# Norm 2's squares summed over four channel blocks on GpSimd before the matmul with ones, and the down product's operands loaded a step earlier through six places

## The chip, the cores and the metric

One core of a Trainium2 chip runs the kernel. The metric is the device time of one execution in microseconds, from three runs of it. Within the core, TensorE (PE; its weight loads are listed apart as PEld), VectorE (DVE), ScalarE (ACT) and GpSimd (POOL) each work through a list of instructions in order; SyncE (SP) issues nearly all DMA transfers, also in order, so a transfer whose place on the chip is not free yet holds back every transfer listed behind it.

## The reference

The reference is one inference step of a hybrid layer on 640 tokens, 128 of context and 512 latent ones, in float32, with D = 2048 channels and a feed-forward width of 5632:

```
h  = rmsnorm(x, norm1_g) * (1 + sc1) + sh1
p  = h @ w_in
o_a, state = bidirectional RWKV-7 scan over p's first part
o_b = chunked gMLP over the rest
x  = x + g1 * (concat(o_a, o_b) @ w_out)
h  = rmsnorm(x, norm2_g) * (1 + sc2) + sh2            # norm 2
ff = (silu(h @ w_ffn_gate) * (h @ w_ffn_up)) @ w_ffn_down
y  = final rmsnorm(x + g2 * ff)
```

where `rmsnorm` divides a token's channels by the root of the mean of their squares. The three outputs are both token streams after the last norm, and the context's scan states. The change touches norm 2 and the last of the products, `@ w_ffn_down`, called the down product here.

## The kernel before, in words

**Products.** Channels lie on partitions and tokens along the free axis. Every float32 operand of a product is split in two: ACT copies the rounded high part (`hi`, L1329 and L163), DVE subtracts it from the operand for the low part (`lo`, L1330 and L164), and TensorE does three matmuls for each 128x128 block of weights: hi by hi, hi by lo, lo by hi (L1511 to L1513 in the feed-forward part, L1364 to L1366 for `w_out`). In the feed-forward part the products are done Strassen's way. For each 2x2 block of weights there are seven products of sums of blocks, taken in the order 1, 2, 3, 7, 5, 6, 4 (`PORD`). GpSimd makes the sums of weights (`combine`, L1424).

**Order of the work.** The kernel is written in a framework whose scheduler sets each engine's order of instructions; buffers are named places in pools, and a load into a place waits until the last reader of what stood there is done.

**Norm 2.** Ahead of it, the product with `w_out` is done for two halves of 320 tokens (`hf`), and within each for 16 blocks m of 128 output channels. A block takes 24 matmuls; then `add_out` (L1012) puts the result into `x1T[m]`, a DMA stores it, ACT squares it (L1375), and one block later TensorE multiplies the squares by a matrix of ones and adds them up in PSUM (`stats`, L1348), 16 times for each half. Each of these calls to `TE.matmul` has two float32 operands and appears as two MATMUL records. At m = 15 `stats` forms the norm's factor `rs` (L1351 to L1353). While the second half is being multiplied, `first_half` applies `rs` to the first: GpSimd multiplies (L1300), DVE scales and shifts (L1302), and the operands of the up product are split (L1290, L1291).

**Up product.** It goes over the blocks f of the feed-forward width, `ORDER` having `NFF` of them, two by two. Each pair's gated activations are stored to HBM as the down product will need them: the sums 1, 2, 7 and 6 whole in `d_op`, the sums 3, 5 and 4 already split in `d_os`.

**Down product.** It runs in six chunks of the feed-forward width (`CHK` = 3, 3, 4, 4, 4 and 4 pairs of blocks) with eight steps n each, a step being the seven products for one pair of output blocks. The seven operands `xd` of a chunk stay on the chip for its eight steps. At the last step of each chunk, called the **turn** here (the end of the up product for chunk 0), `load_ops` brings in the next chunk's operands: `direct` (L1550) loads operands 3, 5 and 4, which are split already; `load` (L1556) loads the others into `opd` tiles of up to two blocks, which go through four places (`stags`), and `part` then splits them, copies on ACT (L1563) and subtractions on DVE (L1564; on GpSimd for the block in `POOLK`). An operand's old `xd` tiles are in use until its product in the turn is done, so a new operand can be put in only behind that product. The steps at which this happens are in `AT` and `BT`: operands 1 and 2 are loaded at product index o = 1 of the turn, 1 is put in and 7 loaded at o = 2, 2 is put in and 6 loaded at o = 4, 7 is put in at o = 6, and 6 at o = 0 of the next chunk's first step. The weights `rawd` (L1535) are loaded two steps ahead through ten places (`wtags`); all of these places are on the same queue, SP's.

## Time and profile before

| | us |
|---|---|
| three runs | 3448.01, 3428.27, 3420.05 |
| median of the runs | 3428.27 |
| the profiled execution, its own time | 3418.51 |
| its span, from the first to the last instruction | 3416.7 |
| PE busy | 3253.2 (95% of the span) |
| DVE busy | 2413.6 (71%) |
| ACT busy | 1449.3 (42%) |
| GpSimd busy | 1239.6 (36%) |

The last four rows are busy times over the whole program and hide that its stages have different limits. The parts that the change touches are two: norm 2, from 1561 to 1690 us of the span, and the six turns, of which the first lies at 2786 to 2812 us and the last at 3245 to 3265. The profile's rows name engine, line, operation and tiles: `lo L1330` is the subtraction that writes the tile `lo` on line 1330. An x and a number is a count, and a tile name ahead of `<-` is what is written.

### The profile page before, as it was taken

To read this page: it belongs to the slowest core of one execution; us is meant where nothing else is said; L and a number is where in the kernel's file an instruction comes from. 1 tells how busy PE (TensorE), PEld (TensorE's weight loads), DVE (VectorE), ACT (ScalarE), POOL (GpSimd) and SP (SyncE) were. 2 spreads that over 40 slices of the span, in tenths; PEclk is the share of its full clock that TensorE was granted. 3 is DMA by queue.
4 is the path that set the end of the run, shared out by engine and by line. 5 is a ranking of instruction groups with operands and counts; after the bars stand their busy time and mean duration, and the time that the engine had idled before them with its cause. 6 is when DMAs were issued, how large, how long until landed. Compare 5 with 4: busy or idle time off the path is not lost.

```text
span 3416.7 us, 72586 instructions
## 1 busy us (share of the span) xinstructions
PE 3253.2 (95%) x28260; PEld 2934.0 (86%) x28260; DVE 2413.6 (71%) x4320; ACT 1449.3 (42%) x3161; POOL 1239.6 (36%) x1090
## 2 busy tenths in 40 slices
PE   6899999999999999999899999999999999999996
PEld 3688777777877887768899999999999999999986
DVE  4547766765866666654887768777777777877787
ACT  3334444434444333323554444444444444443365
POOL 0001121112112103230136565656565655555543
PEclk8899999999999999999999999999999999999998
DMA  8766676766667587644533444343434354543453
GB/s 318 236 186 186 183 190 179 174 173 179 175 185 198 152 251 221 207 143 143 168 116 112 124 121 126 106 127 115 130 103 130 116 173 151 155 148 116 144 167 114
DMA packets 736176, 550.11 MB, mean 161 GB/s; under 512 B 140328, under 2 KB 670008, under 8 KB 727000
## 3 DMA queue, kind: packets, MB, share of 16 engines
q1 hardware_dynamic: 723512, 531.78, 52.3%
q0 software_dynamic: 9984, 13.13, 1.8%
q8 instruction: 222, 3.64, 0.4%
q14 instruction: 122, 1.00, 0.1%
q10 hardware_dynamic: 2336, 0.57, 0.1%
HBM read 436.68 MB, written 111.28 MB: 160 GB/s over the span
## 4 chain that ended last, share of the span: by engine, by line
PE 45%; DVE 4%; issue 4%; DMA 1%; POOL 0%; ACT 0%; DVEq 0%; SPq 0%; POOLq 0%; ACTq 0%
PE P L1513 14%; PE P L1511 14%; PE P L1512 14%; DVE lo L1330 1%; DMA opd<-d_op 1%; DVE xd L1564 1%; PE big L1366 0%; PE big L1364 0%; PE big L1365 0%; DVE xo L1291 0%; DVE out L1867 0%; PE C L1445 0%; PE C L1443 0%; PE C L1444 0%; POOL rawd L1424 0%
## 5 line engine op out<-in xcount | busy, mean ns | idle before, releaser
L1511 PE MATMUL P<-xo,hi 128*128 128x320 f32 x2352 | 727.7, 309 | 3.3 <-ACT hi L1329 3.3
L1513 PE MATMUL P<-xo,lo 128*128 128x320 f32 x2352 | 727.4, 309 | 1.9 <-DVE lo L1330 1.9
L1512 PE MATMUL P<-xo,hi 128*128 128x320 f32 x2352 | 727.4, 309 | 0.0
L1330 DVE TENSOR_TENSOR lo<-raw,hi 128x512 fp32r<-128x512 f32 x532 | 509.1, 960 | 177.1 <-ACT hi L1329 172.3
L1329 ACT CAST hi<-raw 128x512 fp32r<-128x512 f32 x532 | 330.7, 622 | 495.4 <-PE P L1512 399.1
L185 PE MATMUL big<-h_hi,hi 128*128 128x320 f32 x1376 | 456.3, 332 | 9.5 <-ACT hi L163 4.5
L1511 PEld LDWEIGHTS P<-xo,hi 128*128 128x128 f32 x2352 | 442.1, 188 | 3.5 <-ACT hi L1329 3.5
L1513 PEld LDWEIGHTS P<-xo,lo 128*128 128x128 f32 x2352 | 441.9, 188 | 2.3 <-DVE lo L1330 2.3
L187 PE MATMUL big<-h_hi,lo 128*128 128x320 f32 x1376 | 442.9, 322 | 0.7 <-DVE lo L164 0.7
L186 PE MATMUL big<-h_lo,hi 128*128 128x320 f32 x1376 | 441.8, 321 | 0.5 <-DVE h_lo L342 0.5
L1512 PEld LDWEIGHTS P<-xo,hi 128*128 128x128 f32 x2352 | 442.1, 188 | 0.0
L1424 POOL TENSOR_TENSOR raw<-raw 128x512 f32<-128x512 f32 x252 | 409.3, 1634 | 12.7 <-DVE lo L1330 1.1
L1513 PE MATMUL P<-xd,lo 128*128 128x320 f32 x1232 | 385.3, 313 | 17.6 <-DVE lo L1330 17.4
L1511 PE MATMUL P<-xd,hi 128*128 128x320 f32 x1232 | 383.2, 311 | 6.0 <-ACT hi L1329 2.6
L1512 PE MATMUL P<-xd,hi 128*128 128x320 f32 x1232 | 381.9, 310 | 0.0
L164 DVE TENSOR_TENSOR lo<-raw,hi 128x512 fp32r<-128x512 f32 x268 | 185.1, 693 | 247.9 <-ACT hi L163 225.0
L185 PEld LDWEIGHTS big<-h_hi,hi 128*128 128x128 f32 x1376 | 266.8, 194 | 83.3 <-issue 55.2
L163 ACT CAST hi<-raw 128x512 fp32r<-128x512 f32 x268 | 165.4, 619 | 302.5 <-PE big L186 142.6
L186 PEld LDWEIGHTS big<-h_lo,hi 128*128 128x128 f32 x1376 | 267.2, 194 | 17.9 <-issue 12.3
L187 PEld LDWEIGHTS big<-h_hi,lo 128*128 128x128 f32 x1376 | 266.8, 194 | 12.2 <-issue 4.8
L1329 ACT CAST hi<-rawd 128x512 fp32r<-128x512 f32 (+1 forms) x288 | 168.8, 587 | 239.0 <-PE P L1512 203.7
L1513 PEld LDWEIGHTS P<-xd,lo 128*128 128x128 f32 x1232 | 232.4, 189 | 25.5 <-DVE lo L1330 25.3
(358 smaller groups left out, 6288.3 us busy)
## 6 DMA issues: line engine op xcount, KB each, us to landing
wt<-in_w_mod_dram SPq DMA_DIRECT2D x96, 1024.0 KB
raw<-in_w_ffn_gate_dram SPq DMA_DIRECT2D x182, 256.0 KB
raw<-in_w_ffn_up_dram SPq DMA_DIRECT2D x182, 256.0 KB
rec<-d_S SPq DMA_DIRECT2D x80, 576.0 KB
raw<-in_w_in_dram SPq DMA_DIRECT2D x172, 256.0 KB
rawd<-in_w_ffn_down_dram SPq DMA_DIRECT2D x128, 256.0 KB
raw<-in_w_out_dram SPq DMA_DIRECT2D x96, 256.0 KB
xd<-d_os SPq DMA_DIRECT2D x66, 320.0 KB
```

What stands on the lines that cost most here:

```text
L163: S.copy(hi, raw)
L164: V.tensor_sub(lo, raw, hi.bitcast(F32))
L185: TE.matmul(halves[hf], hi[:, k, :], h_hi[:, kb, s], start=(kb == 0), stop=False)
L186: TE.matmul(halves[hf], hi[:, k, :], h_lo[:, kb, s], start=False, stop=False)
L187: TE.matmul(halves[hf], lo[:, k, :], h_hi[:, kb, s], start=False, stop=(kb == KB - 1))
L1329: S.copy(hi[:, 0:nk], raw[:, 0:nk])
L1330: V.tensor_sub(lo[:, 0:nk], raw[:, 0:nk], hi[:, 0:nk].bitcast(F32))
L1424: G.tensor_tensor(out=o[:, 0:nk], in0=p[:, 0:nk], in1=q[:, 0:nk], op=ALU.subtract)
L1511: TE.matmul(ps, hi[:, k, :], xk[:, 0, :], start=f, stop=False)
L1512: TE.matmul(ps, hi[:, k, :], xk[:, 1, :], start=False, stop=False)
L1513: TE.matmul(ps, lo[:, k, :], xk[:, 0, :], start=False, stop=l)
L1564: (G if (k + q) in POOLK else V).tensor_tensor(out=x[:, 1, :], in0=t[:, q, :], in1=x[:, 0, :].bitcast(F32), op=ALU.subtract)
```

## The change

**Norm 2.** `squares` squares a block as before, but adds it on GpSimd to the sum of the blocks before it in its group, and only the group's sum goes to the matmul with ones. The first half has four groups of four blocks. The second has three of four, one of two, and the last two blocks by themselves, so that the end of the half is as before. There are 10 calls to the matmul with ones in place of 32, and 22 additions of 128x320 float32 elements on GpSimd. The tile of squares gets three buffers instead of two.

**Down product.** The operands of chunk 0 are loaded by other means: 1 and 2 one step of the up product earlier (f = `NFF` - 2, o = 6), block by block into the places of the up product's weights (`raw`); 7 and 6 at o = 2 of the last f, into four places of `ftags`, which held operand 3 of the up product until product 3 ended. For the later chunks, operands 1, 2 and 7 are loaded in the step ahead of the turn (`s % 8 == 6`) at o = 2, 3 and 4, through six places instead of four, and 6 at o = 1 of the turn. They are put in at o = 1 (operand 1), 3 (2) and 5 (7) of the turn, ahead of which it was 2, 4 and 6, and 6 at o = 0 of the next chunk's first step as before. `direct(4)` is issued at o = 0 of that step instead of o = 1. The ten places of the weights are the same ones in another order.

```diff
+        four = [range(4 * i, 4 * i + 4) for i in range(4)]
+        GROUPS = (four, four[:3] + [range(12, 14), range(14, 15), range(15, 16)])
+        def squares(hf, m):
+            sq = np_.tile([P, HALF], F32, tag="sq2", name="sq2", bufs=3)
+            S.activation(sq, x1T[m][:, HALF * hf:HALF * hf + HALF], AF.Square)
+            group = next(g for g in GROUPS[hf] if m in g)
+            if m == group[0]:
+                sumq[0] = sq
+            else:
+                total = np_.tile([P, HALF], F32, tag="sumq", name="sumq")
+                G.tensor_tensor(out=total, in0=sumq[0], in1=sq, op=ALU.add)
+                sumq[0] = total
+            if m == group[-1]:
+                sqs.append((hf, m, sumq[0]))
...
-            TE.matmul(ss[hf], ones, sq, start=(m == 0), stop=(m == KB - 1))
+            TE.matmul(ss[hf], ones, sq, start=(m == GROUPS[hf][0][-1]), stop=(m == KB - 1))
...
-                sq = np_.tile([P, HALF], F32, tag="sq2", name="sq2")
-                S.activation(sq, x1T[m][:, s], AF.Square)
-                sqs.append((hf, m, sq))
+                squares(hf, m)
...
-    wtags, stags, ctags = tags(13, 2, 11, 10, 4, 3, 12, 5, 14, 15), tags(8, 1, 0, 9), tags(6, 7, 0, 8)
+    wtags, stags, ctags = tags(13, 10, 4, 15, 3, 12, 14, 5, 2, 11), tags(8, 1, 0, 9, 6, 7), tags(6, 7, 0, 8)
+    ftags = iter(["x1_8", "rs2", "x1_2", "x1_11"])
...
+    def load(c, i):
+        got[i] = []
+        if c == 0 and i < 3:
             for k in range(CHK[c]):
+                t = gu.tile([P, 1, HALF], F32, tag="raw", name="opd", bufs=RAWB)
+                nc.sync.dma_start(t[:, 0, :], d_op[starts[c] + k, i - 1])
+                got[i].append((k, 1, t))
+            return
+        for k in range(0, CHK[c], 2):
+            n = min(2, CHK[c] - k)
+            t = xap.tile([P, 2, HALF], F32, tag=next(stags if c else ftags), name="opd")
...
-        load(1)
-        load(2)
-        yield
-        part(1)
-        load(7)
-        yield
-        part(2)
-        direct(3)
-        load(6)
-        yield
-        part(7)
-        yield
-        direct(5)
-        part(6)
-        yield
-        direct(4)
-        yield
-    AT, BT = (2, 4, 6), (0, 1)
+    FIRST_OPS = {1: ((put_in, 1),), 2: ((put_in, 2), (load, 0, 7), (load, 0, 6), (direct, 0, 3)), 4: ((direct, 0, 5),),
+                 5: ((put_in, 7),), 6: ((put_in, 6), (direct, 0, 4))}
+    def turn_ops(c):
+        return {1: ((put_in, 1), (load, c, 6)), 3: ((put_in, 2), (direct, c, 3)), 5: ((put_in, 7), (direct, c, 5))}
...
+            if f == NFF - 2 and o == 6:
+                load(0, 1)
+                load(0, 2)
             if f == NFF - 1:
-                if o == 1:
-                    ops = load_ops(0)
-                    next(ops)
-                if o in AT:
-                    next(ops)
+                now(FIRST_OPS, o)
...
+            if s % 8 == 6 and c < NC - 1 and o in (2, 3, 4):
+                load(c + 1, (1, 2, 7)[o - 2])
             if turn:
-                if o == 1:
-                    ops = load_ops(c + 1)
-                    next(ops)
-                if o in AT:
-                    next(ops)
-            elif s % 8 == 0 and o in BT:
-                next(ops)
+                now(turn_ops(c + 1), o)
+            elif after and o == 0:
+                put_in(6)
+                direct(c, 4)
```

`put_in` is the `part` of before, and `now` runs the functions that a table lists for o. Lines of the changed kernel have other numbers: L1535 becomes L1552, L1550 L1582, L1556 L1573 (L1567 for the block-by-block loads), L1348 L1366, and L1356 is the new addition.

On **GpSimd in norm 2** the list before, from the end of the scan (`Y`) to the first sums of weights (`t`), was:

```order
L1189 TENSOR_SCALAR ys<-ys 128x10
L132 TENSOR_TENSOR ys<-ys,mhalf 128x10
L1192 TENSOR_TENSOR Y<-Y,ys 128x320 x2
L1300 TENSOR_TENSOR x1T<-x1T,rs_18776 128x320 x16
L1424 TENSOR_TENSOR t_21128<-raw 128x512
L1424 TENSOR_TENSOR raw<-raw 128x512
```

With the change, from block 12 of the first half on (`sumq` is the running sum, `sq` a block's squares):

```order
L1356 TENSOR_TENSOR sumq<-sq_19357,sq_19399 128x320
L1356 TENSOR_TENSOR sumq<-sumq,sq_19443 128x320
L1356 TENSOR_TENSOR sumq<-sumq,sq_19487 128x320
L1300 TENSOR_TENSOR x1T<-x1T,rs_18776 128x320 x6
L1356 TENSOR_TENSOR sumq<-sq_19535,sq_19577 128x320
L1300 TENSOR_TENSOR x1T<-x1T,rs_18776 128x320 x10
L1356 TENSOR_TENSOR sumq<-sumq,sq_19633 128x320
L1356 TENSOR_TENSOR sumq<-sumq,sq_19677 128x320
L1356 TENSOR_TENSOR sumq<-sq_19734,sq_19776 128x320
L1356 TENSOR_TENSOR sumq<-sumq,sq_19832 128x320
L1356 TENSOR_TENSOR sumq<-sumq,sq_19876 128x320
L1356 TENSOR_TENSOR sumq<-sq_19933,sq_19975 128x320
```

Three more additions of the first half's last group now stand ahead of the sixteen multiplications of x1T by `rs`, one of the second half's stands between them, and the rest stand behind.

On **SP's queue at the end of the up product** the list before, from the first weights of the down product (`rawd`) on, was:

```order
L1535 DMA rawd<-in_w_ffn_down_dram 128x3x128
L1672 DMA d_op<-act 128x320
L1610 DMA d_op<-s_33084 128x320
L1535 DMA rawd<-in_w_ffn_down_dram 128x3x128
L1550 DMA xd<-d_os 128x640 x2
L1556 DMA opd<-d_op 128x2x320
L1550 DMA xd<-d_os 128x640 x2
L1556 DMA opd<-d_op 128x320
L1535 DMA rawd<-in_w_ffn_down_dram 128x3x128 x3
L1556 DMA opd<-d_op 128x2x320
L1556 DMA opd<-d_op 128x320
```

With the change it is the following; four of the six loads of single blocks (L1567) stand directly ahead of these rows, among the stores to `d_os` of the pair before:

```order
L1651 DMA d_os<-sp 128x320
L1567 DMA opd<-d_op 128x320
L1651 DMA d_os<-act 128x320
L1567 DMA opd<-d_op 128x320
L1552 DMA rawd<-in_w_ffn_down_dram 128x3x128
L1689 DMA d_op<-act 128x320
L1627 DMA d_op<-s_33131 128x320
L1552 DMA rawd<-in_w_ffn_down_dram 128x3x128
L1582 DMA xd<-d_os 128x640
L1573 DMA opd<-d_op 128x320
L1573 DMA opd<-d_op 128x2x320 x2
L1573 DMA opd<-d_op 128x320
```

The first operands' loads moved ahead of the last activations' stores (`d_op<-act`, L1672 before), behind which they stood. The loads of operands 7 and 6 (L1573) moved from behind three loads of weights to ahead of two of them.

On **SP's queue at the turn from chunk 0 to chunk 1 and the steps behind it** the list before was:

```order
L1535 DMA rawd<-in_w_ffn_down_dram 128x3x128 x21
L1556 DMA opd<-d_op 128x2x320
L1556 DMA opd<-d_op 128x320
L1550 DMA xd<-d_os 128x640 x3
L1556 DMA opd<-d_op 128x2x320
L1556 DMA opd<-d_op 128x320
L1550 DMA xd<-d_os 128x640 x6
L1535 DMA rawd<-in_w_ffn_down_dram 128x3x128 x8
L1556 DMA opd<-d_op 128x2x320 x4
L1535 DMA rawd<-in_w_ffn_down_dram 128x3x128 x16
```

With the change:

```order
L1552 DMA rawd<-in_w_ffn_down_dram 128x3x128 x23
L1573 DMA opd<-d_op 128x2x320
L1573 DMA opd<-d_op 128x320
L1582 DMA xd<-d_os 128x640 x9
L1552 DMA rawd<-in_w_ffn_down_dram 128x3x128 x7
L1573 DMA opd<-d_op 128x2x320
L1552 DMA rawd<-in_w_ffn_down_dram 128x3x128
L1573 DMA opd<-d_op 128x2x320 x5
L1552 DMA rawd<-in_w_ffn_down_dram 128x3x128 x16
```

The loads of operands for the turn after this one stood in a row of four behind this turn's own and the weights of two steps; they now stand in a row of six (one load of weights between the first and the others).

More of the change, by code (lines that the diff above doesn't have):

```diff
@@ L1540, in flow_step @@
     SPLIT = (3, 5, 4)
[L1542 to L1547 removed]
+    got = {}
+    def load(c, i):
+        got[i] = []
+        if c == 0 and i < 3:
             for k in range(CHK[c]):
[L1549 to L1582 removed]
@@ new lines, in new, with direct, put_in @@
+    def new(i, k):
+        return xpool(i, k).tile([P, 2, HALF], F32R, tag=f"xo{i}_{k}", name="xd")
+    def direct(c, i):
+        for k in range(CHK[c]):
+            XD[i, k] = x = new(i, k)
+            nc.sync.dma_start(x.bitcast(F32), d_os[starts[c] + k, SPLIT.index(i)])
+    def put_in(i):
+        for k, n, t in got.pop(i):
+            for q in range(n):
+                XD[i, k + q] = x = new(i, k + q)
+                S.copy(x[:, 0, :], t[:, q, :])
+                (G if (k + q) in POOLK else V).tensor_tensor(out=x[:, 1, :], in0=t[:, q, :],
+                                                           in1=x[:, 0, :].bitcast(F32), op=ALU.subtract)
@@ L1587, in flow_step, with now @@
+    FIRST_OPS = {1: ((put_in, 1),), 2: ((put_in, 2), (load, 0, 7), (load, 0, 6), (direct, 0, 3)), 4: ((direct, 0, 5),),
+                 5: ((put_in, 7),), 6: ((put_in, 6), (direct, 0, 4))}
+    def turn_ops(c):
+        return {1: ((put_in, 1), (load, c, 6)), 3: ((put_in, 2), (direct, c, 3)), 5: ((put_in, 7), (direct, c, 5))}
+    def now(table, o):
+        for fn, *a in table.get(o, ()):
+            fn(*a)
     WB = {}
```

23 lines of the change are left out of this document (3 added, 20 removed).

## The prediction

> **What bounds the kernel now.** I read the page's busy times first, then the busy time of stretches that the change touches, then the waits of the down product and the chain that ended last around its turns.
>
> ```profile
> span 3416.7 us, 72586 instructions
> PE 3253.2 (95%) x28260; PEld 2934.0 (86%) x28260; DVE 2413.6 (71%) x4320; ACT 1449.3 (42%) x3161; POOL 1239.6 (36%) x1090
> core 0: us, PE busy (x) PEld busy (x) DVE busy (x) ACT busy (x) POOL busy (x), PEclk, DMA share, GB/s
> 1561.00:1619.00 58.00, 57.87 (x368) 55.09 (x367) 29.05 (x61) 24.85 (x45) 0.00 (x0) 1.00 0.59 177
> 1624.00:1641.00 17.00, 11.50 (x61) 9.99 (x59) 16.50 (x22) 5.06 (x10) 16.07 (x16) 0.90 0.28 82
> 1641.00:1664.00 23.00, 22.34 (x143) 21.45 (x143) 22.56 (x62) 14.54 (x30) 0.00 (x0) 1.00 0.60 181
> 1760.00:2770.00 1010.00, 1010.00 (x6884) 1010.00 (x6883) 770.83 (x964) 435.29 (x759) 608.30 (x408) 1.00 0.39 118
> 2794.00:2812.00 18.00, 14.08 (x71) 13.04 (x70) 12.09 (x23) 9.10 (x22) 8.19 (x7) 0.81 0.76 240
> 2871.00:2899.00 28.00, 25.16 (x165) 23.84 (x164) 20.23 (x39) 12.64 (x30) 12.70 (x12) 1.00 0.82 259
> 2950.00:2966.00 16.00, 12.90 (x84) 12.11 (x84) 14.85 (x23) 7.63 (x16) 7.77 (x7) 1.00 0.91 299
> 3050.00:3066.00 16.00, 13.99 (x92) 13.14 (x90) 13.63 (x20) 7.73 (x17) 7.41 (x7) 1.00 0.88 307
> 3152.00:3168.00 16.00, 13.83 (x90) 12.88 (x89) 13.45 (x20) 7.71 (x16) 7.03 (x7) 1.00 0.92 323
> 3247.00:3264.00 17.00, 15.70 (x104) 14.91 (x102) 13.69 (x19) 11.82 (x28) 9.67 (x7) 1.00 0.53 168
> ```
>
> TensorE is busy for 95% of the span, so only two things can shorten the program: fewer matmuls, or fewer holes between them. The up product shows the undisturbed rate, 1010 us for 6884 matmuls, 0.1467 us each. That gives a measure for every other stretch: its length less its matmuls times 0.1467 is what it loses. The first half of norm 2 (1561 to 1619) has no holes and DVE idles half of it. In the second half, from 1624 to 1641, TensorE is held up, since DVE works 16.50 of 17 us and GpSimd 16.07. The six turns of the down product lose, in the order of the rows, 18 - 71 x 0.1467 = 7.6 us, then 3.8, 3.7, 2.5, 2.8 and 1.7 us: 22.1 us together. No edit of the operands' loads can bring more than that.
>
> Why do they lose it? The waits from 2777 to 3270 us (us in total, times, longest) and the chain at the first turn:
>
> ```profile
> ACT xd L1563 <- DMA opd<-d_op: 27.5, 18, 3.1
> POOL t L1424 <- DMA rawd<-in_w_ffn_down_dram: 144.8, 34, 6.8
> PE P L1513 <- DVE lo L1330: 12.1, 15, 1.7
> ...
> 2789.02 5.88 DMA opd<-d_op
> ...
> 2794.92 0.47 ACT xd L1563
> ...
> 2804.25 1.55 DVE xd L1564 x2
> 2805.80 0.48 DVE lo L1330
> ...
> 2806.32 0.63 PE P L1513
> ```
>
> ACT stands still 27.5 us in all for operands that are on their way. At the first turn the matmul chain passes into the transfer that begins at 2789.02 and comes back only through ACT's copy and DVE's subtraction. The copy of an operand stands in ACT's list ahead of the copy of the next weights, so what PE then lacks is mostly `lo`, the last product of that row (12.1 us). The later turns are not all of this kind. At the second, it is weights as well; at the third, an operand; at the fourth, no transfer stands in the chain, only DVE, whose subtractions run beside GpSimd's sums of weights:
>
> ```profile
> 2882.02 5.48 DMA rawd<-in_w_ffn_down_dram
> 2892.19 5.88 DMA opd<-d_op
> 2953.86 5.91 DMA opd<-d_op
> 3048.19 1.18 DVE xd L1564
> 3049.70 1.17 DVE xd L1564
> 3051.20 1.35 DVE lo L1330
> 3046.23 4.70 POOL L1424 TENSOR_TENSOR rawd<-rawd 128x512 f32<-128x512 f32 x3
> 3046.67 4.60 DVE L1564 TENSOR_TENSOR xd<-opd,xd 128x320 fp32r<-128x320 f32 x3
> L1564 DVE TENSOR_TENSOR xd<-opd,xd x72: 477/486/1592, 2783.4 to 3266.1; 128x320 fp32r<-128x320 f32 x72
> ```
>
> Three subtractions took 4.60 us while three sums ran on GpSimd, 1.53 each against a median of 0.486.
>
> **Norm 2, part by part.** The rows are those of the matmul with ones (minimum, median and maximum in ns), three of DVE in the first half, and GpSimd's multiplication of the same shape as the new addition.
>
> ```profile
> L1348 PE MATMUL ss<-sq,ones x64: 431/432/537, 1561.2 to 1689.7; 128*128 128x320 f32 x64
> 1610.54 0.68 DVE L1012 SCALAR_TENSOR_TENSOR x1T<-big,modc,x1T 128x256 f32<-128x256 f32 x2 [0.52 <-PE big L1366]
> 1613.39 0.69 DVE L164 TENSOR_TENSOR lo<-raw,hi 128x512 fp32r<-128x512 f32 x1 [1.58 <-ACT hi L163]
> 1614.60 0.68 DVE L1012 SCALAR_TENSOR_TENSOR x1T<-big,modc,x1T 128x256 f32<-128x256 f32 x2 [0.52 <-PE big L1366]
> L1300 POOL TENSOR_TENSOR x1T<-x1T,rs x16: 854/930/1409, 1623.9 to 1638.9; 128x320 f32<-128x320 f32 x16
> 1628.13 0.68 DVE L164 TENSOR_TENSOR lo<-raw,hi 128x512 fp32r<-128x512 f32 x1
> 1630.89 2.63 DVE L164 TENSOR_TENSOR lo<-raw,hi 128x512 fp32r<-128x512 f32 x2
> ```
>
> From 1610.54 to 1614.60 one block goes by, 4.06 us. Its 24 matmuls take 24 x 0.1467 = 3.52, so one call with ones (two records) takes 0.54 us of TensorE's time. The duration of 432 ns in its row is not the cost, since consecutive matmuls overlap. Of 32 calls 22 go: 22 x 0.54 = 11.9 us at most.
>
> Twelve of them lie in the first half, where TensorE alone sets the pace: 12 x 0.54 = 6.5 us, all gained. The additions there run on a GpSimd with nothing else to do, once a block, after the square; an addition of 0.93 us falls into the gap of 1.58 us that DVE has ahead of `lo`, which shrinks to about 1.04 with the shorter block, so it still about fits.
>
> Ten calls, 5.4 us, lie in the second half, and not all come back. About three (1.6 us) stand where DVE is the bound (1624 to 1641), and taking matmuls from an engine that waits gains nothing. About four (2.2 us) stand from 1641 to 1664, where DVE has 22.56 of 23 us to do and any added load on it shows. The additions use DVE's time though they are not DVE's work: beside GpSimd's multiplications `lo` took 2.63 / 2 = 1.32 us instead of 0.68, so an addition costs DVE about 0.63 us if it runs beside one of its subtractions. Ten additions stand there (three groups of four and one of two); if six meet DVE while it is the bound, and half of their time falls on it, 6 x 0.93 / 2 = 2.8 us. No record of before shows this addition, so its price has two ends: nothing (all in DVE's gaps, sum -11.9), and 0.63 for each of ten with the three calls gaining nothing (-11.9 + 1.6 + 6.3 = -4). I take -11.9 + 2.8 = -9.1, rounded to **-9**, since the row of 1641 shows TensorE at 22.34 of 23 us, nearer the case in which its matmuls count.
>
> The Trainium skill speaks against this part: "SBUF — State Buffer", section "SBUF: two separate sides", calls the pair of ports that GpSimd and VectorE share an exclusive lock, which a VectorE operation with two SBUF inputs takes too, the later one waiting for the whole of the other. By that rule an addition in the way would cost up to its full 0.93 us, and the second half would lose 6 x 0.93 = 5.6 us instead of 2.8, the sum being -6. The trace agrees that the two hinder each other (1.32 us against 0.68), and the first rival below says what it does at worst.
>
> Nothing waits newly behind the additions. GpSimd's list has the sixteen multiplications by `rs` in it, and the first half's last sum stands ahead of them, and `rs` waits for the matmul of that sum. Its three additions are spread over three blocks of 3.5 us, and only the last, 0.93 us, comes behind the half's last square, ahead of a matmul that stands most of a block later. The sums of the second half's first group stand behind the sixteen multiplications, but their matmul is due only four blocks later; TensorE does not wait for it. The buffers suffice: a square's tile is read within a block, and there are three.
>
> **The turns, part by part.** The new order does three things: an operand's `opd` tile is there before the turn, so ACT's copy waits for the end of the old operand's product alone; two more places let operand 7 come early too; and the put-in moves ahead by one product. ACT's copy thus waits for TensorE, with the copies of the weights for the product after next behind it. That is a shorter wait than for a transfer of 5.9 us, and the weights in front of it are split already.
>
> At the first turn operands 1 and 2 come out of the way of the last activations' store, and 7 and 6 no longer wait for those operands' places: they are asked for behind product 3, three products ahead of where they came (3 x 24 x 0.1467 = 10.6 us). Both transfers in the chain vanish, and with them the lowered clock of that row (0.81), which follows the hole: 6.5 of 7.6 us. At the second turn the operand goes and the weights stay: 2.0 of 3.8. At the third the operand goes and DVE's doubled subtractions stay: 1.5 of 3.7. At the fourth and the fifth, where DVE beside GpSimd is the chain and operand 6 alone still comes late, 0.3 and 0.6; at the sixth 0.4. Sum 11.3, taken as **-11**. The low end is -20, if ACT's wait was the root of nearly everything; the high end -4, if only the first turn's own wait of some 3 us and the clock behind it are saved.
>
> The rest costs nothing that I can find. Six single loads in place of four double ones are issued on SP in time that SP has. The ten places of weights in another order keep the same distance between loads; what covers them is that a step's weights come two steps ahead, and if that cover were gone, GpSimd's wait for `rawd` (144.8 us, all of it slack now) would reach TensorE, 5.48 us for a load. The move of `direct(4)` by one product has the six products ahead of operand 4's as its cover.
>
> **Sum.** -9 - 11 = -20. Against the profiled execution that is 3418.5 - 20 = 3398.5 us. The four executions shown (3418.5, 3420.05, 3428.27, 3448.01) have a middle of (3420.05 + 3428.27) / 2 = 3424.2, which stands for another set of runs better than the lowest of them: 3424.2 - 20 = **3404 us**, 0.7% below the median.
>
> **The rivals.**
>
> *The additions eat what the matmuls gain.* If each of 22 additions delayed DVE by 0.63 us on the path that sets the end, that is +13.9 against -11.9: norm 2 gives +2, the sum is -9, the time 3415. For it: DVE at 98% from 1641 to 1664. Against it: half of the additions lie where DVE is idle half of the time.
>
> *The transfers were not the bound at the turns.* If DVE beside GpSimd is what costs at all turns but the first, only 4 of 22 us come back: -9 - 4 = -13, 3411. For it the chain at the fourth turn; against it the transfer at 2953.86.
>
> *Everything comes back.* -11.9 - 22.1 = -34, 3390. For it: the doubled subtractions may be a consequence of the late operands, since they then fall together with GpSimd's sums for the next step; put in a product earlier they might miss them. Against it: those sums run 608 of 1010 us in the steady part, so something always meets them.
>
> *Slower: the loads ahead crowd out the weights.* This one has its place in SP's queue behind each later turn.
>
> ```profile
> opd<-d_op SPq DMA_DIRECT2D x40, 320.0 KB
> 2890.63 0.49 SPq L1556
> ```
>
> Before, four loads of 320 KB for the next turn stood there, with the weights of the following step behind; now six, 1.97 MB instead of 1.31. At the 118 GB/s of the steady part six take 16.6 us, four 11.1. If the weights behind them have about 10 us in hand, four turns lose 6.6 us each, 26 us, and with the -20 the sum is +6: 3430. It decides once the rate there falls below 1.97 MB / 10 us = 197 GB/s. At a rate at which six take 21 us (94 GB/s) it would be 44 - 20 = +24, 3448. Against it: 118 GB/s is what was asked for, not what the queue can do; at the turns it moved 259 to 323 GB/s, at which six take 6 to 8 us.
>
> **How the numbers follow.** The forecast 0.50, everything back 0.15, the additions 0.12, the transfers not the bound 0.12, the crowding 0.08, something else 0.03. A measurement of this kernel tells about 1% (34 us) from no change. Below 3394 lie most of "everything back" and a small part of the forecast, 0.19; above 3462 the far end of the crowding and what I have not thought of, 0.07; the rest, 0.74, is within 1%. The range from 3382 to 3432 takes in the terms' low ends (-11.9 - 20 = -32, 3392) with 10 us for the spread between sets of runs, and on the other side the crowding's first price, 3430.
>
> **What would show it.** In norm 2's first half the block would take 3.52 us instead of 4.06, and the records of the matmul with ones would be 20 instead of 64. GpSimd's `sumq` would take about 0.93 us. From 1641 on, `lo` at over 1 us in many blocks and TensorE under 22 us of 23 would speak for the first rival. At the turns ACT's wait for `opd` would fall from 27.5 us to a few, and the first turn's loss from 7.6 to about 1; DVE's `xd` near 1.5 us at the fourth and fifth would stay. If the losses at the turns remain with ACT's wait gone, the second rival is right; if GpSimd's wait for `rawd` ends in waits of TensorE behind a turn, it is the crowding. The forecast is wrong if the time is outside 3382 to 3432, and its mechanism if either part has the other sign.

## The result, and the profile after

The changed kernel took 3401.39 us (median of 18 runs, 3386.64 to 3426.97), the kernel before 3422.65 (18 runs, 3407.41 to 3448.01). The ratio is 0.9949 with a 95% interval of 0.9932 to 0.9965, so it gains 17.5 us (12 to 23). The forecast was 3404 us and a gain of 20. Measured again beside the last experiment the ratio was 0.9939 (0.9923 to 0.9955).

The profiled execution took 3410.02 us, only 8.5 less than that of before, because the stages ahead of the change happened to be slower in it. The first matmul of the product with `w_out` tells it; the first row is of before, the second of after (minimum, median and maximum in ns, then the first and the last start):

```profile
L999 PE MATMUL big<-oh,hi x256: 302/414/417, 1192.0 to 1515.9; 128*128 128x320 f32 x128
```
```profile
L999 PE MATMUL big<-oh,hi x256: 302/414/417, 1203.6 to 1527.6; 128*128 128x320 f32 x128
```

All code ahead of that line is the same, and it begins 11.6 us later. In the fourteen profiles of this study it begins between 1180 and 1204 us, so two single executions can't be set against each other by their spans; below, only stretches behind it are compared. From the second half of the `w_out` product on (1518.6 and 1530.4 us) to the end of the span the two profiles differ by 20.3 us. Not all of that is the change: 48.1 - 44.3 = 3.8 us of it lie between these two points and the result of norm 2's third block, where TensorE was granted less of its clock before than after:

```profile
core 0: us, PE busy (x) PEld busy (x) DVE busy (x) ACT busy (x) POOL busy (x), PEclk, DMA share, GB/s
1518.60:1566.70 48.10, 37.71 (x310) 29.02 (x309) 17.21 (x37) 10.89 (x28) 11.01 (x14) 0.79 0.28 87
```
```profile
1530.40:1574.70 44.30, 33.31 (x308) 26.68 (x308) 17.02 (x38) 11.04 (x28) 13.90 (x16) 0.88 0.31 94
```

The traces of all fourteen profiles have such stretches, of 3.4 us or a multiple of it, in which the granted clock (PEclk) is 0.50, called half clock below. Their places differ from profile to profile, so below it is said where one falls into a stretch that is compared.

**Norm 2.** Of the changed kernel, the matmul with ones, the additions, four blocks of the first half on DVE, and the two ends of the second half, where DVE forms the reciprocal of `rs`:

```profile
L1366 PE MATMUL ss<-sumq,ones x16: 431/432/537, 1577.0 to 1684.1; 128*128 128x320 f32 x16
L1356 POOL TENSOR_TENSOR sumq<-sumq,sq x14: 857/882/1322, 1572.3 to 1674.3; 128x320 f32<-128x320 f32 x14
L1356 POOL TENSOR_TENSOR sumq<-sq,sq x8: 879/998/2442, 1570.3 to 1681.9; 128x320 f32<-128x320 f32 x8
```
```profile
1606.54 0.68 DVE L1012 SCALAR_TENSOR_TENSOR x1T<-big,modc,x1T 128x256 f32<-128x256 f32 x2 [0.52 <-PE big L1384]
...
1621.16 0.68 DVE L1012 SCALAR_TENSOR_TENSOR x1T<-big,modc,x1T 128x64 f32<-128x64 f32 x2 [0.52 <-PE big L1384]
1624.15 2.15 DVE L1371 RECIPROCAL rs<-rs 128x320 f32<-128x320 f32 x1 [1.32 <-ACT rs L1370]
1691.25 2.15 DVE L1371 RECIPROCAL rs<-rs 128x320 f32<-128x320 f32 x1 [0.54 <-ACT rs L1370]
```

Four blocks of the first half now take 1621.16 - 1606.54 = 14.62 us, against 4 x 4.06 = 16.24: 1.62 less, three calls of 0.54. From the third block's result to the sixteenth's it is 1618.66 - 1566.72 = 51.94 us before and 1621.16 - 1574.68 = 46.48 after, 5.46 less for ten calls fewer:

```profile
1566.72 0.68 DVE L1012 SCALAR_TENSOR_TENSOR x1T<-big,modc,x1T 128x256 f32<-128x256 f32 x2
1618.66 0.68 DVE L1012 SCALAR_TENSOR_TENSOR x1T<-big,modc,x1T 128x64 f32<-128x64 f32 x2 [0.52 <-PE big L1366]
```
```profile
1574.68 0.67 DVE L1012 SCALAR_TENSOR_TENSOR x1T<-big,modc,x1T 128x256 f32<-128x256 f32 x2
```

The other two of the twelve calls lie in the first three blocks, which the clock makes differ by more than their 1.1 us. An addition takes 0.88 us in the median (the larger of the two groups) and up to 2.44 where DVE is busy. The second half lasts 67.10 us from reciprocal to reciprocal. Before it was 69.5:

```profile
1621.66 2.15 DVE L1353 RECIPROCAL rs<-rs 128x320 f32<-128x320 f32 x1 [1.33 <-ACT rs L1352]
1691.19 2.15 DVE L1353 RECIPROCAL rs<-rs 128x320 f32<-128x320 f32 x1 [0.54 <-ACT rs L1352]
```

**The turns.** The changed kernel's stretch around its first turn, and its waits from 2777 to 3270 us:

```profile
core 0: us, PE busy (x) PEld busy (x) DVE busy (x) ACT busy (x) POOL busy (x), PEclk, DMA share, GB/s
2796.00:2820.00 24.00, 20.52 (x129) 18.71 (x128) 18.11 (x31) 10.87 (x25) 12.10 (x11) 1.00 0.75 242
```
```profile
POOL t L1440 <- DMA rawd<-in_w_ffn_down_dram: 143.7, 34, 6.5
...
PE P L1529 <- DVE lo L1330: 9.3, 11, 1.7
ACT xd L1588 <- DMA opd<-d_op: 6.5, 5, 3.4
```

ACT's wait for operands has fallen from 27.5 to 6.5 us and the dip of the clock at the first turn (0.81) is gone, but the stretch still loses 24 - 129 x 0.1467 = 5.1 us. Before, that dip was two stretches of half clock:

```profile
2799.30:2802.70 3.40, 3.40 (x15) 3.40 (x14) 1.46 (x3) 0.93 (x3) 3.24 (x4) 0.50 0.74 229
2806.10:2809.50 3.40, 3.17 (x12) 3.18 (x13) 2.14 (x5) 0.77 (x2) 0.96 (x1) 0.50 0.81 248
```

For the comparison of kernels the losses below are taken from the matmuls' starts, each product's length less its matmuls times 0.1467, summed over the steps around each turn (the first turn: the first three steps; the sixth: the last two steps of its chunk and the first of the next; the others: the last step and the three behind it). "Mean before" is over the four profiles with the old loads (the kernel before, e1, e3 and e4 of the experiments), "mean after" over the four with the new ones and the same turns (the changed kernel, e2, e10 and e12). The rows on half clock are an estimate of the part that the clock has in it: for the matmuls that start while 0.50 was granted, what each takes beyond 0.1467 us, at most another 0.1467.

| us lost at the turn | 1 | 2 | 3 | 4 | 5 | 6 | sum |
|---|---|---|---|---|---|---|---|
| mean before | 8.3 | 4.2 | 4.0 | 2.8 | 3.0 | 3.7 | 26.0 |
| of it half clock | 2.0 | 0.4 | 0 | 0 | 0 | 0 | 2.4 |
| mean after | 5.0 | 3.2 | 2.5 | 2.5 | 2.8 | 3.0 | 19.0 |
| of it half clock | 0 | 0 | 0 | 0 | 0.4 | 0 | 0.4 |
| predicted gain | 6.5 | 2.0 | 1.5 | 0.3 | 0.6 | 0.4 | 11.3 |
| gain | 3.3 | 1.0 | 1.5 | 0.3 | 0.2 | 0.7 | 7.0 |

(26.0 is more than the 22.1 of the prediction because these stretches are longer, and because nine other matmuls at the sixth turn, 1.3 us, count as loss both before and after.) Of the first turn's 3.3 us, 2.0 are thus half clock that is gone and only 1.3 shorter waits; all four profiles with the old loads have half clock there, the four with the new ones none, and why is not shown. The gains at the first, third and sixth turn are clear of the spread between profiles. That at the second is not: the turn lost 2.7 to 5.7 before and 2.9 to 3.6 after. Nor is that at the fifth, 2.6 to 3.4 before and 2.5 to 3.7 after.

The whole down product, from its first to its last matmul, took 595.5 us on average with the old loads and 586.9 with the new ones, 8.6 less; the 1.7 beyond the turns lie in the last chunk's steps behind its first (27.4 to 25.7 us lost, of which 17.3 are other matmuls of TensorE's there).

### The profile page after: what moved, and what is told of

It is laid out like the page before. It is cut to its first block, busy times and chain, and to the rows that moved or that the text cites. A ratio compares the mean times of both kernels' runs of the same rounds, so it can differ in the third digit from the quotient of the medians.

```text
span 3408.2 us, 72541 instructions
## 1 busy us (share of the span) xinstructions
PE 3249.5 (95%) x28216; PEld 2934.2 (86%) x28216; DVE 2411.4 (71%) x4320; ACT 1450.7 (43%) x3161; POOL 1263.0 (37%) x1112
## 4 chain that ended last, share of the span: by engine, by line
PE 76%; DVE 11%; issue 4%; DMA 4%; POOL 2%; ACT 2%; SPq 0%; DVEq 0%; ACTq 0%; POOLq 0%
PE P L1529 15%; PE P L1527 14%; PE P L1528 14%; PE big L185 4%; PE big L187 4%; PE big L186 4%; PE pG L624 3%; PE pm L869 2%; PE big L999 2%; DMA raw<-in_w_in_dram 1%; DVE lo L1330 1%; DMA wt<-in_w_mod_dram 1%; PE big L1382 1%; PE big L1384 1%; PE pmm L496 1%
## 5 line engine op out<-in xcount | busy, mean ns | idle before, releaser
L1529 PEld LDWEIGHTS P<-xd,lo 128*128 128x128 f32 x1232 | 231.2, 188 | 20.4 <-DVE lo L1330 20.3
```

The costliest lines, as they stand in the source:

```text
L1529: TE.matmul(ps, lo[:, k, :], xk[:, 0, :], start=False, stop=l)
```

## The experiments

### Each part alone

```diff
 e1_norm2: the hunks on squares, GROUPS and stats alone
 e2_loads: all other hunks alone
```

> Norm 2's part of the change alone, the operands' loads as before. If the matmuls with ones set the pace and the additions hide: about -9 us, a ratio near 0.9974; the blocks of norm 2's first half in a rhythm of 3.82, 3.76, 3.52, 3.52 us in place of 4.06, the second half some 3 us shorter, and the six turns losing 22 us as before. If the additions eat the gain: no change (within 0.05%), the second half longer than before.

> The down product's part of the change alone, norm 2 as before. If the two parts are independent: what the trace of the whole change shows in the down product, about -10 us (the stretch from its first to its last matmul 586 us instead of 596), a ratio near 0.997, norm 2 with 4.06 us a block. If part of that gain came through norm 2 or through chance: less than 5 us.

Norm 2's part alone gave a ratio of 0.9975 (0.9956 to 0.9993), 8.5 us; the loads alone 0.9981 (0.9963 to 1.0), 6.5 us, which by time alone is not clear of nothing. Together that is 15, within the interval of the whole change's 17.5. In the profiles the parts are independent: with the first, norm 2's second half is 67.1 us and the turns lose 25.1; with the second, the half is 68.9, the turns lose 18.6, and the down product takes 587.1.

### The price of the additions and of the calls

```diff
 e3_adds_extra, on the kernel before:
+                group = next(g for g in GROUPS[hf] if m in g)
+                if m == group[0]:
+                    sumq[0] = sq
+                else:
+                    total = np_.tile([P, HALF], F32, tag="sumq", name="sumq")
+                    G.tensor_tensor(out=total, in0=sumq[0], in1=sq, op=ALU.add)
+                    sumq[0] = total
 e4_no_adds, on e1_norm2:
             else:
-                total = np_.tile([P, HALF], F32, tag="sumq", name="sumq")
-                G.tensor_tensor(out=total, in0=sumq[0], in1=sq, op=ALU.add)
-                sumq[0] = total
+                sumq[0] = sq
```

> The kernel before with the 22 additions on GpSimd put in beside all 32 calls with ones; nothing reads the sums, so this prices the additions alone. If they hide: first half at 4.06 us a block as before, the second half up to 1 or 2 us longer where DVE is the bound (its blocks 2 to 4). If each one delays DVE by 0.63 us on the path: some 6 us longer in the second half and several in the first.

> The change's norm 2 with 10 calls with ones, but without the additions: only the last square of each group is counted, so three quarters of the sum of squares is left out. Loads as before. If the additions hide: the same rhythm as with them in the first half, and at most 1 or 2 us less in the second. If they cost on the path: second half some 6 us shorter than with them.

The second half's ends, of the kernel with additions and all calls, and of the one with 10 calls and no additions, which leaves the other blocks' squares out of the sum:

```profile
1614.72 2.15 DVE L1355 RECIPROCAL rs<-rs 128x320 f32<-128x320 f32 x1 [1.33 <-ACT rs L1354]
1685.20 2.15 DVE L1355 RECIPROCAL rs<-rs 128x320 f32<-128x320 f32 x1 [0.54 <-ACT rs L1354]
```
```profile
1616.69 2.15 DVE L1369 RECIPROCAL rs<-rs 128x320 f32<-128x320 f32 x1 [1.33 <-ACT rs L1368]
1681.79 2.15 DVE L1369 RECIPROCAL rs<-rs 128x320 f32<-128x320 f32 x1 [0.54 <-ACT rs L1368]
```

| second half, us | 32 calls | 10 calls |
|---|---|---|
| without additions | 69.5 and 68.9 | 65.1 |
| with additions | 70.5 | 67.1 |

Taking the calls away is worth 4.1 us of the 5.4 counted (69.2 to 65.1), even though DVE bounds part of this half. The ten additions cost 2.0 us beside 10 calls and 1.3 beside 32. The kernels with 70.5 and with 65.1 were profiled once each; with 10 calls and the additions the half took 67.1 or 67.2 in all ten profiles, and with 32 calls and no additions 69.5 and 68.9, so the 1.3 is the less certain price. In the first half, blocks 4 to 15 had the same rhythm with and without additions (3.82, 3.76, 3.52, 3.52, and 4.06 with all calls), so the additions there are free. That bears out the prediction's reading, with a price of 0.13 to 0.20 us for an addition in the crowded half. The rival in which every addition costs 0.63 is out: it asked for 6 us.

### Other places for the second step's weights, and the last splits put off

At the first turn two things could hold TensorE up. The chain of the changed kernel there:

```profile
2801.20 1.19 POOL act L1630
...
2803.97 1.16 DVE act L1649
2805.13 0.48 DVE lo L1330
2805.61 0.33 SPq L1651
...
2805.99 0.45 SPq L1552
...
2807.55 4.78 DMA rawd<-in_w_ffn_down_dram
...
2812.49 0.98 POOL t L1440
...
2816.30 0.93 DVE lo L1330
```

DVE stands before the splits of the up product's last sums (L1649), which GpSimd makes (L1630) only behind its sums of the next weights; the stores of those splits (L1651) stand in SP's queue, with weights of the down product's second step among and behind them (L1552). The first costs step 0, the second step 1: 2.9 and 2.4 us here.

```diff
 e5_places:
-    wtags, stags, ctags = tags(13, 10, 4, 15, 3, 12, 14, 5, 2, 11), tags(8, 1, 0, 9, 6, 7), tags(6, 7, 0, 8)
+    stags, ctags = tags(8, 1, 0, 9, 6, 7), tags(6, 7, 0, 8)
+    wtags = itertools.chain([f"x1_{j}" for j in (13, 10, 4, 15, 3, 12, 1, 9)], tags(14, 5, 2, 11, 13, 10, 4, 15, 3, 12))
 e9_defer:
...
-    part(3)
...
+            if s == 3 and o < 3:
+                part(1, ("x1_0", "x1_9", "x1_1")[o])
```

> The changed kernel with other places for two of the down product's second step's weights: in the first round of the ten they take x1_1 and x1_9, which held operands 7 and 6 of the up product, instead of x1_14 and x1_5, which the last gate still uses. If the weights of that step come late at the first turn because their place comes free late and they then stand behind the last stores: the 2.4 us lost in step 1 go, and the first turn loses about 3 us instead of 5.4. If the transfers' rate or GpSimd's sums hold them up: it still loses about 5.

> The changed kernel with the splits and stores of the up product's last three sums (act<-act,sp on DVE, sp on ACT, six stores) put off from the first turn into the down product's fourth step; they are not read before its last chunk. If what is left at the first turn is DVE standing before these splits, which wait for GpSimd behind its sums of weights, with the weights' low parts behind them in DVE's list and the second step's weights behind the stores in SP's: the first turn loses 3 us or less instead of 5.4. If the transfers or GpSimd's sums themselves set it: it still loses about 5.

In these two profiles the first turn lost 5.8 and 5.0 us, no less than in the changed kernel. With the other places step 1 lost 0.35 us instead of 2.4, but step 0 5.4 instead of 2.9: DVE waits 1.73 us for GpSimd's sum of activations, and its splits and low parts behind that are stretched, as GpSimd, whose weights are there sooner, is at the second step's sums by then:

```profile
2792.79 0.49 DVE L1650 TENSOR_TENSOR act<-act,sp 128x320 fp32r<-128x320 f32 x1 [1.73 <-POOL act L1631]
2793.20 1.22 DVE L1330 TENSOR_TENSOR lo<-rawd,hi 128x384 fp32r<-128x384 f32 x1
2794.35 1.28 DVE L1650 TENSOR_TENSOR act<-act,sp 128x320 fp32r<-128x320 f32 x1
2795.55 2.50 DVE L1330 TENSOR_TENSOR lo<-rawd,hi 128x384 fp32r<-128x384 f32 x2
```

With the splits put off, step 0 lost 1.3, and step 1, whose weights still came late, 3.7. So my expectation of 3 us missed in both. But each of the two profiles has 3.4 us of half clock in the step that lost more, the first row in step 0 with the other places, the second in step 1 with the splits put off:

```profile
2794.40:2797.80 3.40, 3.32 (x12) 3.21 (x13) 3.40 (x4) 0.13 (x1) 3.15 (x3) 0.50 0.74 254
```
```profile
2812.70:2816.10 3.40, 3.40 (x15) 3.40 (x14) 1.75 (x4) 1.31 (x4) 0.03 (x1) 0.50 0.62 177
```

By the estimate of the table that is 1.4 and 1.5 us, and without it the turn lost about 4.3 and 3.5, against 4.8 to 5.4 in the four profiles with the changed kernel's loads, which have no half clock there. So the other places gain 2 us in step 1 and cost about 1 in step 0; the deferred splits gain about 1.6 in step 0 and leave step 1 as it was. Whether the edits bring the half clock about or it fell there by chance, one profile of each can't tell.

### DVE's subtractions at the later turns

```diff
 e6_late_put:
-        return {1: ((put_in, 1), (load, c, 6)), 3: ((put_in, 2), (direct, c, 3)), 5: ((put_in, 7), (direct, c, 5))}
+        return {3: ((put_in, 1), (load, c, 6), (direct, c, 3)), 4: ((put_in, 2),), 5: ((put_in, 7), (direct, c, 5))}
...
+                if e is V and i in later_turns:
+                    tc.keep_in_program_order(late)
 e8_gpsimd_two:
-POOLK = (3,)
+POOLK = (2, 3)
```

> The changed kernel with DVE's subtractions of the later turns' operands held in the written order and put in at o = 3, 4 and 5, behind the products during which GpSimd makes the next sums of weights. If what is left at the turns is DVE's subtractions stretched by GpSimd's sums (1.5 us each instead of 0.49): each of turns 2 to 5 falls from 2.5 or 2.9 us to below 1, the sum of the six from 19 to about 12. If it is the number of subtractions on DVE wherever they stand: they lose 2 us and more as they do now.

> The changed kernel with two of four blocks of each operand subtracted on GpSimd instead of one (POOLK = (2, 3)), so that DVE has two stretched subtractions ahead of the weights' low part instead of three. If DVE's stretched subtractions are what is left: turns 4 and 5 lose about 1 us (2.5 less one subtraction of 1.5). If GpSimd's sums of weights become the bound: they lose more than 2.5, with PE waiting for copies of weights behind GpSimd's.

The changed kernel at the fourth turn, DVE and GpSimd, and then the same place with the subtractions held back:

```profile
3042.45 4.60 DVE L1589 TENSOR_TENSOR xd<-opd,xd 128x320 fp32r<-128x320 f32 x3
3042.01 4.69 POOL L1440 TENSOR_TENSOR rawd<-rawd 128x512 f32<-128x512 f32 x3
```
```profile
3032.36 2.66 DVE L1590 TENSOR_TENSOR xd<-opd,xd 128x320 fp32r<-128x320 f32 x3
3036.24 1.28 DVE L1590 TENSOR_TENSOR xd<-opd,xd 128x320 fp32r<-128x320 f32 x3
3027.26 4.63 POOL L1440 TENSOR_TENSOR rawd<-rawd 128x512 f32<-128x512 f32 x3
3031.85 2.42 POOL L1590 TENSOR_TENSOR xd<-opd,xd 128x320 fp32r<-128x320 f32 x2
```

Three subtractions and three sums go in step, 1.53 and 1.56 us each; alone, three subtractions take 1.28. Held back, the first three still run beside GpSimd's own subtractions and take 2.66, all others 1.28. Turns 3 to 6 lose 1.7, 1.1, 1.1 and 1.7 us instead of 2.8, 2.5, 2.5 and 2.9: the cause is shown, though none fell below 1 as expected. The second turn did not improve (3.7), and the last chunk lost 28.4 us in this profile instead of 24.8 (3.4 us of half clock at 3262, some 1.5 us, are in it), so that the down product as a whole is only 0.8 us shorter (585.2).

With two blocks on GpSimd the turns lose 24.7 us in all, 2.9 at the fourth and fifth instead of 2.5, so the gain of one subtraction did not come. At the second and third it is 5.1 and 5.0, of which some 1.5 each are half clock (at 2860.0 and 2941.9). That GpSimd's sums become the bound, as the rival has it, is not what the chain at the fourth turn shows: DVE stands in it as before, and GpSimd, whose six subtractions now take 7.13 us beside DVE's, does not. Two rows of the chain, and GpSimd's:

```profile
3040.09 1.36 DVE lo L1330
3042.72 1.09 DVE xd L1589 x2
```
```profile
3037.41 7.13 POOL L1589 TENSOR_TENSOR xd<-opd,xd 128x320 fp32r<-128x320 f32 x6
```

That the subtractions and the sums go in step is also what the Trainium skill ("SBUF — State Buffer", section "SBUF: two separate sides") says: a VectorE operation with two SBUF inputs waits for the whole of GpSimd's operation and not for a share of it. The trace agrees for back-to-back operations (1.53 beside 1.56 us); for the single additions of norm 2 the full wait was not paid on the path.

### Four places instead of six

```diff
 e7_four:
-    wtags, stags, ctags = tags(13, 10, 4, 15, 3, 12, 14, 5, 2, 11), tags(8, 1, 0, 9, 6, 7), tags(6, 7, 0, 8)
+    wtags, stags, ctags = tags(13, 10, 4, 15, 3, 12, 14, 5, 2, 11), tags(8, 1, 0, 9), tags(6, 7, 0, 8)
...
-        return {1: ((put_in, 1), (load, c, 6)), 3: ((put_in, 2), (direct, c, 3)), 5: ((put_in, 7), (direct, c, 5))}
+        return {1: ((put_in, 1), (load, c, 7)), 3: ((put_in, 2), (load, c, 6), (direct, c, 3)), 5: ((put_in, 7), (direct, c, 5))}
...
-            if s % 8 == 6 and c < NC - 1 and o in (2, 3, 4):
-                load(c + 1, (1, 2, 7)[o - 2])
+            if s % 8 == 6 and c < NC - 1 and o in (2, 3):
+                load(c + 1, (1, 2)[o - 2])
```

> The changed kernel with four places for operands instead of six: 1 and 2 still loaded in the step ahead of the turn, 7 behind the put-in of 1 and 6 behind that of 2. If it is the earlier load of the first operands that helps, and 7 and 6 come in time through four places: turns 2 to 6 within 0.5 us of those of the changed kernel (2.9, 2.8, 2.5, 2.5, 2.9). If the two further places are what helps: they lose what they lost before (4.2, 4.0, 2.8, 3.0 and 3.7 us on average).

The turns lost 4.9, 3.9, 2.7, 2.5, 2.5 and 2.9 us. So the two further places are not what helps at turns 3 to 6; they bring at most some 0.7 us, at the second turn (one profile, 3.9 against a mean of 3.2). What is left there is the earlier load of the first two operands and the put-in one product earlier, and no run takes these two apart. The held-back subtractions speak for the load: there operand 1 is put in at o = 3, later than the 2 of before, and the turns lose least.

### Wider sums, and all that helped together

```diff
 e10_wide:
-        GROUPS = (four, four[:3] + [range(12, 14), range(14, 15), range(15, 16)])
+        GROUPS = ([range(16)], [range(12), range(12, 14), range(14, 15), range(15, 16)])
 e11_both: e5_places + e9_defer + e6_late_put, and
+        GROUPS = ([range(16)], four[:3] + [range(12, 14), range(14, 15), range(15, 16)])
 e12_again: the changed kernel
```

> The changed kernel with wider groups in norm 2: all sixteen blocks of the first half in one sum, and twelve, two, one and one in the second, so 5 calls with ones instead of 10 and 27 additions instead of 22. If the price of a call is TensorE's 0.54 us wherever TensorE is the bound: the first half some 1.6 us shorter (3.52 us in nearly every block), the second up to 1.1 shorter, with at most 0.5 us for the further additions. If the longer chain of additions on GpSimd holds the norm's factor up: a longer block at the halves' border.

> Four edits together on the changed kernel: the other places for the second step's weights and the splits of the last sums put off (the two of the first turn), DVE's subtractions of the later turns held behind GpSimd's sums, and one sum over all sixteen blocks in norm 2's first half. If the first turn's loss has these two causes, each of which showed the other when it was taken away alone (3.7 us left in step 1, 5.4 in step 0): it falls to about 2 us now. Turns 2 to 6 as with the late put-in alone (9.4 us), norm 2's first half 1.8 us shorter. Together some 9 us below the changed kernel, a ratio near 0.992 to the kernel before. If the first turn is set by the transfers: it keeps 5 us, and the ratio is 0.993 or more.

> The changed kernel itself once more, beside the one with the four edits on the same chip: a ratio to the kernel before of 0.993 to 0.9965, as measured at first, and the losses at the six turns as in its first profile (5.4, 2.9, 2.8, 2.5, 2.5, 2.9) if they are the program's and not chance.

With one sum over sixteen blocks the first half's blocks 4 to 15 take 3.52 us each, all that the calls had cost is gone, and 1.8 us are gained, where 1.6 were expected; the second half stayed at 67.2 us, so there the two calls fewer, 1.1 us, gained nothing.

With the four edits the first turn lost 2.8 us, and no half clock fell into it; the other seven profiles with new loads that have none there lost 4.8 to 5.7. So the two edits together do gain, some 2 us, and both causes are real; by the estimate above (about 0.7 and 1.5 us alone) the two simply add up, and that one hides the other is not shown. The deferred splits cost 2.0 us at the fifth step instead, a stretch outside the table. Turns 2 to 6 lost 4.2, 1.8, 1.2, 1.4 and 1.8. Its time was 3395.63 us (5 runs, ratio 0.9931, 0.9915 to 0.9946), that of the changed kernel beside it 3401.10 (0.9939, 0.9923 to 0.9955). It has the lowest median of the kernels that ran more than once, but the intervals overlap: by time the two aren't told apart, and the 9 us expected did not come. The down product, 584.6 against 587.5 us, says why: of 7 us gained at the turns, 2.0 went to that fifth step and 2.1 to the last chunk (27.3 instead of 25.2).

In the changed kernel's second profile the turns lost 4.9, 3.6, 2.5, 2.5, 3.7 and 2.9: its fifth differs by 1.2 us from the first profile, and it is the one with half clock in it, from 3148.4 to 3151.8 us.

## Why the prediction was right, point by point

**The rate and the bounds.** The loss of a stretch as its length less 0.1467 us a matmul held in all profiles: the steps between the turns lose 0.0 us by it, those with the deferred splits aside. What it does not tell is whether a loss is a wait or the clock.

**The time.** The gain of 20 came out as 17.5 (12 to 23), each of its two terms somewhat smaller than forecast. That 3404 lies within 3 us of 3401.39 is in part luck: the medians differ by 21.3, more than the gain by ratio, and the 3424.2 that the forecast starts from happened to be near the median of the 18 runs, 3422.65.

**Norm 2, -9.** Measured 8.5 us by time (2 to 15); by stretches 5.5 in the first half and 2.1 in the second (69.2 to 67.1). In the first half the price of a call, 0.54 us, and the free additions are as predicted; ten of the twelve calls are measured, and whether the other two came back, 1.1 us, can't be told. In the second the prediction had 5.4 - 2.8 = 2.6: the price of the additions was sized at 2.8, and they cost 2.0, while the calls brought 4.1 and not 5.4. Both errors were under 1.5 us and opposite, so that 2.1 comes near 2.6 is partly luck. The prediction's step that weighed what DVE would have to bear was right in kind.

**The turns, -11.** Measured 7.0 at the turns. Turns 3, 4 and 6 came as worked out (1.5, 0.3 and 0.7 against 1.5, 0.3 and 0.4), the last two small beside the spread between profiles. The term that was mis-sized is the first turn's, "Both transfers in the chain vanish, and with them the lowered clock of that row": 6.5 of 7.6 us. Transfers and lowered clock do vanish, and 3.3 us came back, 2.0 of them the clock and 1.3 waits. What the prediction did not ask there is what is late next: the last activations' splits on DVE, behind GpSimd, and the stores of them in front of the second step's weights on SP. Both stood in the chain of before, behind the transfers' part that the prediction quoted:

```profile
2803.84 0.04 DVE act L1632
...
2807.17 0.32 SPq L1634
...
2807.54 2.73 DMA rawd<-in_w_ffn_down_dram
```

At the second turn 1.0 of 2.0 came back, within the spread of its profiles, and the weights' lateness there remains.

**What was not in the sum.** The last chunk's 1.7 us. What it loses varies from 24.7 to 28.4 between profiles, mostly in its second step, where DVE waits for the residual (`cd` on `x1d`), and two of the profiles have some 1.5 us of half clock in it. Whether the change has a part in it stays open.

**The rivals.** The additions did not eat the gain. Part of that rival's sign did show: in the 23 us that match the prediction's row of 1641, TensorE was busy under 22 us and DVE all the time, while `lo` stayed at 0.68 us in all but the first block; what the additions cost is the 2.0 above.

```profile
1643.50:1666.50 23.00, 21.60 (x140) 20.75 (x141) 23.00 (x54) 14.49 (x30) 5.99 (x6) 1.00 0.60 179
```

The second rival (the transfers were not the bound) is half right: 7 of 26 us came back, or 5 without the half clock, between its 4 and the forecast's 11, and its reason, DVE beside GpSimd, is what remained at turns 3 to 6. The crowding did not show: GpSimd waits 143.7 us for weights, before 144.8, and behind turns 3, 4 and 5 the next chunk's first steps lose nothing.

## What to carry to other kernels

Price a stall by its stretch, length less matmuls times the undisturbed rate, and then ask of each stall that goes what stands next in the lists of the same engines; at the first turn 6.5 us were forecast for two transfers and the clock behind them, and 2.0 came back as clock and 1.3 as shorter waits. A small reduction done by matmul in float32 is dear where TensorE is the bound, and summing first on an idle engine is nearly all gain, as long as that engine's partner, here DVE beside GpSimd, is idle too. Where an edit is worth a microsecond or two, look at the granted clock of the stretch before its profile is read as no gain: by the estimate above, 3.4 us of half clock hid what each of two edits had gained at the first turn.

## What the runs showed of the hardware

DVE's subtraction and GpSimd's sum of two tiles each go in step when both have several behind one another: 1.53 us for a subtraction that takes 0.43 alone (1.28 for three).

The granted clock falls to 0.50 for 3.4 us or a multiple of it. The first blocks of the up product, the same in all kernels, take 61.2 to 61.4 us in nine of the fourteen profiles and 62.7 to 63.0 in five, of kernels with norm 2's part and without. The five are those with 3.4 us of half clock inside these blocks, in four of them at 1692 to 1700 us. In the changed kernel, the fifth, the granted clock was 0.88 from 1740 to 1754 us and 71 matmuls kept TensorE busy for 12.06 us; before it was 1.00, and 10.61, so such a stretch costs about 1.5 us where TensorE sets the pace:

```profile
1740.00:1754.00 14.00, 10.61 (x71) 10.03 (x69) 14.00 (x24) 7.17 (x17) 7.55 (x4) 1.00 0.40 116
```
```profile
1740.00:1754.00 14.00, 12.06 (x71) 11.67 (x70) 14.00 (x23) 7.13 (x17) 7.66 (x4) 0.88 0.40 119
```

In norm 2's second half, which DVE bounds in part, a further such stretch cost nothing: with one just behind the half's start (the changed kernel) and with two in a row (its second profile, and norm 2's part alone) the half took 67.1 us. What sets off the lower clock was not tested.
